# A streaming-encoder block: the memory's projections moved to the front, and one seven-product form for the whole first feed-forward

## The chip, the cores and the metric

The kernel runs on one core of one Trainium2 chip. The metric is the device time of one execution in microseconds (us). The kernel before takes 2411.06 us, the median of three runs (2410.53 to 2412.25). Of one execution there is also a trace from the hardware profiler, in which the core's engines are named PE (matrix products; its weight loads are PEld), DVE (the vector engine), ACT (the scalar engine), POOL and SP. SP issues most of the transfers from memory, POOL a few.

## The reference

One layer is computed, in float32, on 256 tokens of 2048 features (`x`), with 256 memory tokens (`mem`):

```
x += 1/2 * SwiGLU(norm(x))                                  # first feed-forward, 2048 -> 2 x 5632 -> 2048
proj = norm(x) @ w_in                                       # mixer: two recurrences and their gates
x += (sigmoid(gate_A)*y_A + sigmoid(gate_B)*y_B) @ w_out
h, m = norm(x), norm(mem)                                   # cross attention, 4 heads of 512
q = h @ wq ;  k, v = split(m @ wkv)
x += concat_heads(softmax(q k^T / sqrt(512)) v) @ wo
x += 1/2 * SwiGLU(norm(x))                                  # second feed-forward
out = norm(x)

SwiGLU(h): gate, up = split(h @ w_up);  (silu(gate) * up) @ w_down
```

The keys and values depend on `mem` and `wkv` alone, so their place in the program is free up to the attention.

## The kernel before

**Split products.** Each float32 operand is split into a high part, which PE multiplies at its fast rate, and a low part, the remainder. A product of two tiles is three matmuls (high by high, high by low, low by high). For each weight tile (128 x 2048, a *piece*, 1 MB) ACT copies out the high part (L154, `h`) and DVE subtracts it from the raw tile (L155, `l`). The results of matmuls, each 512 columns wide in the feed-forwards, gather in eight banks (`acc`).

**The feed-forward.** The hidden width of 5632 is cut into 11 groups of 512. A group's up-projection has eight pieces, p0 to p7, each of 256 input features by 1024 columns (gate and up). A piece covers a two by two block of tiles for each of the operands, and there are several forms for it:

- *plain* and *mixed*: eight products, 24 matmuls; DVE makes one low part of 2048 columns.
- *fast*: seven products, 21 matmuls, on sums and differences of the blocks (a scheme like Strassen's). The weights' differences are made first (L327 to L331 and L341, `td`); then the raw part of 1536 columns and two halves of the differences (1024 columns each) are split into high and low (L154, L155, `l` and `tl`).
- *fast early*: the same with the differences partly in the raw tile's place.
- *fast added*: as fast, but the low part of 1536 columns is made by ACT (the negated high part, L336) and an adding DMA of POOL, so that DVE makes only the differences and their low parts.
- *ready*: the differences were made earlier, kept in DRAM and come back by a DMA in place of a quarter of the raw piece. They are made by `make_ahead` beside other stages: a load by POOL into `prep`, four subtractions (L218), a store by POOL.

A group's down-projection has four pieces of 24 matmuls, each for a block of 512 output columns; some are *added* (DVE makes no low part for them). Groups 1 and 2 are accompanied by two down pieces each, later groups by four. At a group's end DVE and ACT add up the banks (L700 to L712), scale and multiply gate and up (L646), PE turns the result (eight transposes, L653), and ACT and DVE split it (L657, L658, `hidop`). A finished pair of output tiles is added to `x` on DVE (L728).

The table `FIRST` gives the forms and the order of the pieces of the first feed-forward: group 0 is plain, groups 1 and 2 are half mixed, group 3 has two mixed (their low part by an adding DMA), groups 4 to 10 are fast with four added. In the second, all pieces are fast but two of group 0, and `sums_ready` names 56 that are ready.

**The order.** One list, `plan`, holds every weight piece in the order in which PE uses it: first feed-forward, mixer (`in`, `v`, `gate`, `ab`, `out`), `q` (16 column pieces), `k` (16), `mv` (the values, 16 row pieces of 24 matmuls), `o` (16), second feed-forward. `weights` prepares up to two pieces ahead of their use, and `head`, `rest` and `beside` issue other work at given indices of the list: at the opening the operands of `x` are prepared with the first pieces. A column piece (`product`, L360 and L363) has 16 matmuls of 512 and 16 of 256 columns, and its result is summed by ACT (`lo`, L397) and DVE (L399). A row piece is `rows_product` (L385 to L388). Each engine executes its own instructions in the program's order, and waits in that order. The attention's scores and softmax run as generators that are pumped, a step at a time, beside the value pieces.

## Time and profile before

| | us |
|---|---|
| median of three runs | 2411.06 (2410.53 to 2412.25) |
| the profiled execution, its span | 2408.3 |
| PE busy | 2398.9 (100%) |
| DVE busy | 2049.8 (85%) |
| ACT busy | 1467.9 (61%) |
| POOL busy | 100.4 (4%) |

The span reaches from the first to the last instruction of the profiled execution; the median lies 2.76 us above it. A row of a group of instructions reads: line, engine, operation, result <- operands, shape, xcount | busy time in all, mean duration in ns | idle time before them and what ended it. A row of a timeline starts with the start and the duration in us. Durations of neighbouring instructions on PE and DVE overlap, so the distance between two starts is what an instruction occupies of its engine. Line numbers are those of the kernel whose profile is shown; after the change a line has another number (L154 and L155 become L147 and L148, L397 and L399 L407 and L409, L613 and L615 L603 and L605, L327 to L331 and L341 L334 to L338 and L348).

### The profile page before, as it was taken

Reading aid. Unit: us, or ns where it says so; the run is one execution under the profiler, and the core shown is the slowest. Engines: PE = TensorE matmul, PEld = TensorE weight load, DVE = VectorE, ACT = ScalarE, POOL = GpSimd, SP = SyncE. Lnnn points to the kernel's source line nnn. Section 1 sums busy time; section 2 is a strip of 40 time slices with the busy share of each in tenths; the row PEclk is TensorE's granted clock in tenths of the full one; section 3 lists DMA queues with packets and bytes.
Section 4 is the critical chain, followed back from the end, with each engine's and each line's share of the span. In section 5 each row is a group of like instructions: output and inputs, shape, how many; then the busy total and the mean of one; then the engine's idle time right before and its main releaser. Section 6 shows DMA issues by size and latency. Waiting matters only on the chain.

```text
span 2408.3 us, 30805 instructions
## 1 busy us (share of the span) xinstructions
PE 2398.9 (100%) x12098; PEld 2002.8 (83%) x12098; DVE 2049.8 (85%) x2291; ACT 1467.9 (61%) x1502; POOL 100.4 (4%) x162
## 2 busy tenths in 40 slices
PE   9999999999999999999999999999999999999998
PEld 8888888888888888888888888888888888888887
DVE  7999999999866878689777777677799999999995
ACT  8567777777654454476434555545676666666664
POOL 0000000000000000000000000000000000000000
PEclk9999999999999999999999999999999999999999
DMA  8578999999858776878999889876688877787873
GB/s 318 194 234 254 277 276 278 277 272 273 270 215 317 276 283 247 299 286 313 350 339 343 334 334 335 322 282 221 212 319 318 295 279 284 268 292 271 293 281 143
DMA packets 101666, 678.57 MB, mean 282 GB/s; under 512 B 11280, under 2 KB 11792, under 8 KB 29072
## 3 DMA queue, kind: packets, MB, share of 16 engines
q1 hardware_dynamic: 78624, 517.99, 57.7%
q0 software_dynamic: 22752, 158.35, 22.0%
q8 instruction: 95, 1.56, 0.3%
q14 instruction: 51, 0.42, 0.1%
q10 hardware_dynamic: 144, 0.26, 0.0%
HBM read 615.73 MB, written 60.82 MB: 281 GB/s over the span
## 4 chain that ended last, share of the span: by engine, by line
PE 98%; DVE 1%; DMA 0%; ACT 0%; issue 0%; ACTq 0%
PE acc L613 36%; PE acc L615 18%; PE acc L360 11%; PE acc L385 8%; PE acc L386 8%; PE acc L388 8%; PE acc L363 6%; PE acc L653 1%; PE acc L528 1%; DVE tl L155 0%; DVE l L155 0%; PE acc L989 0%; DMA raw<-wd 0%; PE acc L1288 0%; PE acc L1242 0%; PE acc L1104 0%
## 5 line engine op out<-in xcount | busy, mean ns | idle before, releaser
L154 ACT ACTIVATE h<-raw 128x2048 fp32r<-128x2048 f32 (+3 forms) x572 | 862.8, 1533 | 616.1 <-PE acc L386 217.7
L155 DVE TENSOR_TENSOR l<-raw,h 128x2048 fp32r<-128x2048 f32 (+2 forms) x405 | 832.7, 2058 | 226.0 <-ACT h L154 224.4
L613 PE MATMUL acc<-h,xh 128*128 128x512 f32 x1220 | 474.7, 391 | 0.1
L613 PE MATMUL acc<-h,xl 128*128 128x512 f32 x1220 | 472.7, 390 | 0.0
L613 PE MATMUL acc<-h,hidop 128*128 128x512 f32 x1408 | 352.6, 391 | 0.3 <-ACT h L154 0.3
L385 PE MATMUL acc<-h,ops 128*128 128x512 f32 x832 | 326.5, 392 | 0.0
L386 PE MATMUL acc<-h,ops 128*128 128x512 f32 x832 | 324.2, 390 | 0.0
L613 PEld LDWEIGHTS acc<-h,hidop 128*128 128x128 f32 x1408 | 262.5, 188 | 54.5 <-ACT h L154 1.0
L360 PE MATMUL acc<-ops,h 128*128 128x512 f32 x1152 | 277.6, 392 | 0.0
L613 PEld LDWEIGHTS acc<-h,xh 128*128 128x128 f32 x1220 | 229.0, 188 | 52.8 <-ACT h L154 4.7
L613 PEld LDWEIGHTS acc<-h,xl 128*128 128x128 f32 x1220 | 229.1, 188 | 46.5
L360 PEld LDWEIGHTS acc<-ops,h 128*128 128x128 f32 x1152 | 211.4, 188 | 41.4
L155 DVE TENSOR_TENSOR tl<-raw,h 128x1024 fp32r<-128x1024 f32 x167 | 197.4, 1217 | 12.1 <-ACT h L154 11.6
L154 ACT ACTIVATE h<-td 128x1024 fp32r<-128x1024 f32 x145 | 151.8, 1055 | 88.9 <-DVE td L327 35.3
L388 PE MATMUL acc<-l,ops 128*128 128x512 f32 x832 | 206.0, 389 | 0.0
L615 PE MATMUL acc<-l,hidop 128*128 128x512 f32 x704 | 190.6, 389 | 0.0
L385 PEld LDWEIGHTS acc<-h,ops 128*128 128x128 f32 x832 | 156.2, 188 | 32.3
L388 PEld LDWEIGHTS acc<-l,ops 128*128 128x128 f32 x832 | 156.1, 188 | 32.4
L155 DVE TENSOR_TENSOR tl<-td,h 128x1024 fp32r<-128x1024 f32 x145 | 175.9, 1218 | 8.3 <-ACT h L154 7.4
L386 PEld LDWEIGHTS acc<-h,ops 128*128 128x128 f32 x832 | 156.3, 188 | 31.4
L615 PE MATMUL acc<-tl,xh 128*128 128x512 f32 x624 | 177.4, 391 | 0.0
L615 PE MATMUL acc<-l,xh 128*128 128x512 f32 x600 | 165.1, 390 | 0.0
(264 smaller groups left out, 2487.7 us busy)
## 6 DMA issues: line engine op xcount, KB each, us to landing
raw<-wu SPq DMA_DIRECT2D x116, 1024.0 KB, 6.4
raw<-wd SPq DMA_DIRECT2D x88, 1024.0 KB, 6.8
prep<-wu POOLq DMA_DIRECT2D x56, 1024.0 KB, 6.8
t<-prep POOLq DMA_DIRECT2D x56, 1024.0 KB, 5.7
raw<-t SPq DMA_DIRECT2D x56, 1024.0 KB, 6.9
raw<-wu SPq DMA_DIRECT2D x56, 768.0 KB, 4.8
raw<-win SPq DMA_DIRECT2D x40, 1024.0 KB, 5.0
raw<-wg SPq DMA_DIRECT2D x32, 1024.0 KB, 5.5
```

The source lines that it names most:

```text
L154: done["high"] = act.activation(h, raw, ACT.Copy).ins
L155: done["low"] = dve.tensor_tensor(out=l, in0=raw, in1=h.bitcast(F32), op=ALU.subtract).ins
L360: pe.matmul(acc, h[:, k * P:(k + 1) * P], xs[k], start=k == 0, stop=False)
L363: done["product"] = pe.matmul(acc[:, :T], l[:, k * P:(k + 1) * P], xs[k][:, :T], start=False, stop=k == KT - 1).ins
L385: pe.matmul(accs[t], x[:, t * P:][:, :P], h[j], start=first and j == 0, stop=False)
L386: pe.matmul(accs[t], x[:, T + t * P:][:, :P], h[j], start=False, stop=False)
L388: done["product"] = pe.matmul(accs[t], x[:, t * P:][:, :P], l[j], start=False, stop=last and j == 3).ins
L528: pe.transpose(acc[:, z * T + t * P:][:, :P], tile[:, t * 512 + (2 * y + z) * P:][:, :P], ident)
L613: pe.matmul(acc, a, b, start=start, stop=False)
L615: pe.matmul(acc, ah, bl, start=False, stop=stop)
L653: pe.transpose(acc[:, z * T + t * P:][:, :P], hid[t][:, (2 * y + z) * P:][:, :P], ident)
```

## The change

The value and key products of the memory stand at the head of the plan. The memory's operands are prepared at the opening, in place of those of `x`; `x` is loaded and its pairs and sums are prepared behind the first value pieces. The keys, the values and the memory's scale are written to DRAM by POOL, and read back for each head in the attention. All 11 groups of the first feed-forward have the same order of fast and added pieces; in groups 1, 2 and 4 to 9 one fast piece is ready, its differences made beside the value and key products. The first two pieces are fast early. In the second feed-forward 50 pieces in place of 56 are ready. The attention of a head is pumped beside the query products and the output products, whose order (`OUT_ORDER`) lets the first two output blocks start before the last head is done. The pools of the first feed-forward change from three to four wide tiles.

```diff
-FIRST = [
-    "p0 p1 p2 p3 p4 p5 p6 p7",
-    "m0 f1 m2 f3 f5 m4 f7 m6",
-    "m0 f1 m2 f3 f5 m4 f7 m6",
-    "f1 f3 M0 f4 f2 M6 f5 f7",
-    "f1 a3 f0 a4 f2 a5 a6 f7",
...
-KINDS = {"p": "plain", "m": "mixed", "M": "mixed", "f": "fast", "a": "fast"}
+PIECES = "f1 a3 f0 a4 f2 a5 a6 f7"
+FIRST = [PIECES.replace("f2", "r2") if g in (1, 2, 4, 5, 6, 7, 8, 9) else PIECES for g in range(NG)]
...
 def sums_ready(name, e):
-    made = {0:(),1:(6,),2:(5,7),3:(5,7)}.get(e[1], (0, 5, 7) if e[1] % 2 else (0, 3, 5, 7))
+    if name == "ffn1":
+        return e[0] == "fast" and f"r{e[2]}" in FIRST[e[1]]
+    made = {0: (), 1: (5, 7), 2: (3, 5, 7), 3: (3, 5, 7)}.get(e[1], (0, 3, 5, 7))
     return name == "ffn2" and e[0] == "fast" and e[2] not in made
...
+    for g in range(4):
+        plan_rows("mv", wvm, g)
+    plan_columns("k", wk, range(KT))
+    first_ffn = len(plan)
     plan_ffn("ffn1", wu1, wd1)
...
     plan_columns("q", wq, range(KT))
-    plan_columns("k", wk, range(KT))
-    for name, w in (("mv", wvm), ("o", wo)):
-        for g in range(4):
-            plan_rows(name, w, g)
+    for g, kq in OUT_ORDER:
+        plan.append((("o", g, kq), wo[g, kq], "plain"))
...
+        if i < first_ffn:
+            if made_first:
+                turn[0] = i + 3 if len(made_first) > 1 else first_middle + 2
+                steps = make_ahead(*made_first.pop(0))
+                next(steps)
+                under_way.append((i + 2, steps))
...
+    rest[8] = load_vectors
+    for q in range(4):
+        rest[9 + 5 * q] = lambda q=q: load_x(q)
+        rest[11 + 5 * q] = lambda q=q: pairs_x(q)
+        rest[12 + 5 * q] = lambda q=q: (sums_x(0), load_residual(q))
+        rest[13 + 5 * q] = lambda: sums_x(1)
...
+    def keep_values():
+        if not root_of:
+            nc.gpsimd.dma_start(kept_r, sqm.rstd())
+            root_of["mem"] = sqm.rstd_tokens()
+        g, accs = values.pop(0)
+        for t in range(2):
+            f, s = slot(name="vf")[:, :512], slot(F32R, "vs")
+            act.activation(f, accs[t], ACT.Copy, scale=root_of["mem"][:, t:t + 1])
+            split(s[:, :512], s[:, 512:], f)
+            nc.gpsimd.dma_start(kept_v[2 * g + t], s)
+
+    with scope(mem=6, tmp=6, tmp2=1, norms=1, prep=1):
+        for g in range(4):
+            values.append((g, [bank(), bank()]))
+            for kq in range(4):
+                rows_product(values[-1][1], ms.tiles, weights("mv", g, kq), 4 * kq, kq == 0, kq == 3, g == kq == 0)
+            if g:
+                keep_values()
+        ks = Operands()
+        for m in range(KT):
+            ks.add(summed(product(ms.tiles, weights("k", m))[0]))
+            if not m:
+                keep_values()
+            if m % 2:
+                nc.gpsimd.dma_start(kept_k[m // 2], ks.cur)
+
     with scope(**FFN1_POOLS):
         ffn("ffn1", pairs1, sq1, to_mix)
```

The first place where the order moves is DVE's queue at the start of the first feed-forward. Before, the kernel opens with it: `raw` is a piece of weights, `xf` and `xg` are `x`, and each piece gives only its low part (L155).

```order
L300 TENSOR_SCALAR h_179<-raw_168 128x512
L753 SCALAR_TENSOR_TENSOR xl_175<-xf_172,xh_174 128x256
L302 TENSOR_TENSOR l_180<-raw_168,h_179 128x512
L155 TENSOR_TENSOR l_180<-raw_168,h_179 128x512
L753 SCALAR_TENSOR_TENSOR xl_175<-xf_172,xh_174 128x256
L155 TENSOR_TENSOR l_180<-raw_168,h_179 128x512 x2
L155 TENSOR_TENSOR xl_201<-xg_171,xh_200 128x512
L155 TENSOR_TENSOR l_206<-raw_204,h_205 128x512 x4
```

After the change it follows the last key column. `raw_1774` and `raw_1844` are the first two pieces, `acc_1790` is the bank of the last key column, and L409 and L433 make its sum and its low part.

```order
L336 TENSOR_TENSOR raw_1774<-raw_1774,td_1776 128x512
L148 TENSOR_TENSOR tl_1785<-td_1776,h_1784 128x1024
L348 TENSOR_TENSOR raw_1774<-raw_1774 128x512
L409 TENSOR_TENSOR sum_1825<-acc_1790,lo_1823 128x256
L336 TENSOR_TENSOR raw_1844<-raw_1844,td_1846 128x512
L148 TENSOR_TENSOR l_1850<-raw_1844,h_1849 128x1536
L148 TENSOR_TENSOR tl_1785<-raw_1774,h_1784 128x1024
L433 TENSOR_TENSOR ops_1771<-sum_1825,ops_1771 128x256
L348 TENSOR_TENSOR raw_1844<-raw_1844 128x512
L148 TENSOR_TENSOR tl_1855<-td_1846,h_1854 128x1024
L334 TENSOR_TENSOR td_1890<-raw_1888 128x1024
L148 TENSOR_TENSOR tl_1855<-raw_1844,h_1854 128x1024
```

The key column's sum stands in the queue ahead of the second low half of the first piece and of nearly all of the second piece's work.

The second place is DVE's queue where group 0 ends and group 1 begins. Before, group 0 is plain: its end (L646) stands among the last of `x`'s sums (L583, `xs`), and the next pieces are a fast and a mixed one (`raw_599`, `raw_670`).

```order
L327 TENSOR_TENSOR td_601<-raw_599 128x1024
L583 TENSOR_TENSOR xs_615<-xg_433 128x128
L329 TENSOR_TENSOR td_601<-raw_599,td_601 128x512
L583 TENSOR_TENSOR xs_615<-xg_433 128x128
L646 SCALAR_TENSOR_TENSOR ev_589<-acc_219,rtok_591,ev_589 128x512
L646 SCALAR_TENSOR_TENSOR ev_589<-acc_220,rtok_591,ev_589 128x512
L331 TENSOR_TENSOR td_601<-raw_599,td_601 128x512
L155 TENSOR_TENSOR tl_610<-td_601,h_609 128x1024
```

After the change, group 0 is fast and ends with the sums of its seven banks (L690 to L701):

```order
L338 TENSOR_TENSOR td_2112<-raw1_2110,td_2112 128x512
L690 TENSOR_TENSOR ev_2150<-acc_1865,ev_2150 128x512
L334 TENSOR_TENSOR td_2170<-raw_2168 128x1024
L148 TENSOR_TENSOR tl_2121<-td_2112,h_2120 128x1024
L512 RECIPROCAL rtok_2152<-stdt_2151 128x2
L691 TENSOR_TENSOR ev_2150<-acc_1864,ev_2150 128x512
L698 TENSOR_TENSOR ev_2150<-acc_1861,ev_2150 128x512
L698 TENSOR_TENSOR ev_2150<-acc_1863,ev_2150 128x512
L701 TENSOR_TENSOR ev_2150<-acc_1866,ev_2150 128x512
L698 TENSOR_TENSOR ev_2150<-acc_1862,ev_2150 128x512
L701 TENSOR_TENSOR ev_2150<-acc_1863,ev_2150 128x512
L636 SCALAR_TENSOR_TENSOR ev_2150<-ev_2150,rtok_2152 128x512 x2
```

Between the end of one piece's low parts and the next piece's differences there now stand seven additions that group 0 did not have before.

More of the change, by code (lines that the diff above doesn't have):

```diff
@@ L386, in rows_product @@
             pe.matmul(accs[t], x[:, T + t * P:][:, :P], h[j], start=False, stop=False)
-        for x, t, j in terms:
+            if by_tile and j < 3 and t:
+                for y in range(2):
+                    pe.matmul(accs[y], x[:, y * P:][:, :P], l[j], start=False, stop=False)
+        for x, t, j in terms[6:] if by_tile else terms:
             done["product"] = pe.matmul(accs[t], x[:, t * P:][:, :P], l[j], start=False, stop=last and j == 3).ins
@@ L470, in rstd_tokens @@
             return r
[L473 removed]
+    FFN1_POOLS = dict(wide=4, hd=1, raw1=1)
     FFN2_POOLS = dict(wide=2, raw2=2, hid=1, hd=1)
@@ L597, in block_kernel, with three @@
     held = []
-    def three(products, last=0, hold=False, early=0):
+    def three(products, last=0, hold=False):
         high = [(acc, ah, bh, start) for acc, (ah, al), (bh, bl), start, _ in products]
         low = [(acc, al, bh, False) for acc, (ah, al), (bh, bl), _, _ in products]
-        if early:
-            for i in range(0, len(high), 2):
-                for acc, a, b, start in high[i:i + 2] + low[i:i + 2]:
-                    pe.matmul(acc, a, b, start=start, stop=False)
-                if i < early:
-                    for acc, (ah, _), (_, bl), _, _ in products[i:i + 2]:
-                        pe.matmul(acc, ah, bl, start=False, stop=False)
-            high, low, products = [], [], products[early:]
         for acc, a, b, start in [m for pair in zip(high, low) for m in pair]:
@@ L785, in head_residual @@
-    def head_residual(i):
-        for c in (2 * i, 2 * i + 1):
-            for t in range(2):
-                sp.dma_start(xt[c][:, t * 512:(t + 1) * 512], xin[t * P:(t + 1) * P, c * 512:(c + 1) * 512])
-            sq1.add(c, by_vector=c == 3)
-        if i:
-            sp.dma_start(vt[:, small_n:NVEC], vec[:, small_n:])
-    head += [lambda p=p: head_x(p) for p in range(8)]
-    def early_sums():
-        scaled(xq[0][1], opening[0][:, 16:], gain1, 0)
-        for which in ((1, "sums"), (0, "less")):
-            sums1[0]((which,))
@@ L1297, in to_ffn @@
         out = []
-        sums2.append(operand_pairs(turned(xt[c]), gain2, c, slot(name="xg"), out, every=True))
+        sums2.append(operand_pairs(turned(xt[c]), gain2, c, slot(name="xg"), out, differences=True))
         pairs2.extend(out)
@@ L1308, in to_ffn_half @@
             out3.append([])
-        sums = operand_pairs(turned(xt[3], [y]), gain2, 3, *out3, every=True)
+        sums = operand_pairs(turned(xt[3], [y]), gain2, 3, *out3, differences=True)
         pairs2.append(out3[1][-1])
```

329 lines of the change are left out of this document (156 added, 173 removed), and 6 rows, old and new, of the table FIRST.

## The prediction

> **What bounds the kernel now.** I read the page's totals and slices first, then the waits of TensorE (PE), then the stretches of the first feed-forward, then single instructions.
>
> ```profile
> span 2408.3 us, 30805 instructions
> PE 2398.9 (100%) x12098; PEld 2002.8 (83%) x12098; DVE 2049.8 (85%) x2291; ACT 1467.9 (61%) x1502; POOL 100.4 (4%) x162
> PE   9999999999999999999999999999999999999998
> DVE  7999999999866878689777777677799999999995
> PEclk9999999999999999999999999999999999999999
> PE warm L143 <- DVE ones L140: 1.1, 1, 1.1
> PE acc L607 <- DVE h L300: 0.3, 1, 0.3
> PE acc L613 <- ACT h L154: 0.3, 1, 0.3
> ```
>
> PE is busy in every slice at full clock, and its three waits sum to 1.7 us. So time falls only by the matmuls that go away. The DVE row is nearly as full in both feed-forwards, and that is the second bound. The median of the runs, 2411.06, lies 2.76 above the profiled span, 2408.3; I sum against the span and add 2.76 at the end. Here are stretches of the first feed-forward (columns: length, PE, weight loads, DVE, ACT, POOL, clock, DMA share, GB/s), then two of the second:
>
> ```profile
> 60.00:107.00 47.00, 47.00 (x207) 38.46 (x207) 46.90 (x54) 25.82 (x22) 0.00 (x0) 1.00 0.54 202
> 107.00:166.00 59.00, 59.00 (x269) 48.57 (x268) 58.19 (x62) 36.59 (x32) 1.01 (x1) 1.00 0.61 203
> 226.00:287.00 61.00, 61.00 (x273) 49.84 (x272) 59.94 (x63) 46.02 (x39) 4.36 (x5) 1.00 0.90 275
> 287.00:348.00 61.00, 61.00 (x272) 49.96 (x271) 59.72 (x62) 44.14 (x37) 4.36 (x5) 1.00 0.92 276
> 1760.00:1820.00 60.00, 60.00 (x270) 49.59 (x270) 56.83 (x57) 40.68 (x38) 0.00 (x0) 1.00 0.83 308
> 1820.00:1880.00 60.00, 59.95 (x272) 49.30 (x271) 58.38 (x55) 41.59 (x39) 0.00 (x0) 1.00 0.81 303
> ```
>
> From 60 to 166 us (groups 1 and 2, four eight-product pieces and four seven-product pieces each) DVE is busy 105.1 of 106 us, and PE waits for nothing. Seven products there would give DVE more work and PE less time to hide it.
>
> **Prices.** A 512-column matmul costs PE its spacing, not its duration; from the chain of waits:
>
> ```profile
> 10.77 3.63 PE acc L613 x16
> 14.40 1.81 PE acc L615 x8
> ...
> 211.28 1.03 PE L653 MATMUL acc<-vt,ev 128*128 128x128 f32 x8
> 212.07 2.07 PE L613 MATMUL acc<-h,hidop 128*128 128x512 f32 x8
> ```
>
> 3.63/16 = 0.227 us; a piece of 24 is 5.45, one of 21 is 4.77. The 8 transposes of a group take 212.07 − 211.28 = 0.79. For DVE the starts of back-to-back instructions:
>
> ```profile
> 232.64 1.22 DVE L327 TENSOR_TENSOR td<-raw 128x1024 f32<-128x1024 f32 x1
> 233.77 1.75 DVE L155 TENSOR_TENSOR l<-raw,h 128x1536 fp32r<-128x1536 f32 x1
> 235.44 1.22 DVE L155 TENSOR_TENSOR tl<-td,h 128x1024 fp32r<-128x1024 f32 x1
> 236.58 0.69 DVE L329 TENSOR_TENSOR td<-raw,td 128x512 f32<-128x512 f32 x1
> 237.18 1.22 DVE L155 TENSOR_TENSOR tl<-td,h 128x1024 fp32r<-128x1024 f32 x1
> ...
> 254.54 2.28 DVE L155 TENSOR_TENSOR l<-raw,h 128x2048 fp32r<-128x2048 f32 x1
> 256.74 1.22 DVE L155 TENSOR_TENSOR tl<-td,h 128x1024 fp32r<-128x1024 f32 x1
> ```
>
> Start to start: 1.14 (1024 wide), 1.67 (1536), 0.60 (512), 2.20 (2048). A piece then costs DVE:
> - plain or mixed: one low part, 2.21
> - fast: differences 1.14 + 0.60 + 0.60, low parts 1.67 + 2 × 1.14, together 6.29
> - fast added (1536 low part left to POOL's DMA): 4.62
> - ready (differences loaded): 1.67 + 2.28 = 3.95
>
> A group's end adds seven sums (0.60) and two scaled products (0.66), 5.52, and two low parts of the turned hidden operand, 1.20: 6.72. Two finished output columns add four residual additions, 2.40. (Means of the groups below, less the 0.08 by which each start precedes the end before it.)
>
> ```profile
> L709 DVE TENSOR_TENSOR ev<-acc,ev 128x512 f32<-128x512 f32 x30 | 19.6, 680 | 0.0
> L646 DVE SCALAR_TENSOR_TENSOR hid<-hd,rtok,hid 128x512 f32<-128x512 f32 x22 | 15.4, 741 | 0.0
> L658 DVE TENSOR_TENSOR hidop<-acc,hidop 128x512 fp32r<-128x512 f32 x44 | 28.5, 682 | 1.2 <-ACT hidop L657 0.9
> L728 DVE SCALAR_TENSOR_TENSOR x<-acc,x 128x512 f32<-128x512 f32 x96 | 63.8, 682 | 23.0 <-PE acc L615 22.9
> ```
>
> Check on a steady group of before: 43.64 (four fast, four added) + 6.63 (three of four down pieces, one being added) + 6.72 + 2.40 = 59.39; the trace has 59.94 and 59.72.
>
> A page speaks against these prices: the Trainium skill, "VectorE: DVE Perf Modes", section "The DRAIN you can't avoid", says that the next instruction starts only when the pipe is empty, so the full durations (2.28 for 2.20, 1.22 for 1.14) would count. For some 213 instructions at about 0.08 that would be an estimated 17 us more stall. The spacing in these rows disagrees, and the row decides.
>
> **What the change removes.** Group 0 loses a product in 8 pieces, groups 1 and 2 in 4 each, group 3 in 2: 18 pieces × 3 = 54 matmuls × 0.227 = **−12.3 us** on PE, the binding engine. The memory's value and key products are moved, 32 pieces with the same matmuls: 0.
>
> **What it adds on DVE.** In the new order DVE's queue holds the sum of the last key column ahead of most of the second feed-forward piece's work. DVE goes in order, so however idle it was under the keys, it can begin the rest only when PE has finished that column, after ACT's copy (0.38) and DVE's sum (0.33):
>
> ```profile
> L397 ACT ACTIVATE lo<-acc 128x256 f32<-128x256 f32 x96 | 35.9, 377 | 6.8 <-PE acc L1243 6.1
> L399 DVE TENSOR_TENSOR sum<-acc,lo 128x256 f32<-128x256 f32 x72 | 29.6, 416 | 0.0
> ```
>
> From there to the last low part of group 3, DVE has: rest of the first two pieces 0.60 + 1.67 + 1.14 + 0.33 + 0.60 + 2.28 = 6.62, rest of group 0 (three fast, three added) 32.73, its end 6.72, group 1 (three fast, four added, one ready) 41.30, two down pieces with a group's end and residuals 13.54, group 2 41.30 + 13.54, group 3 (none ready) 43.64 and one down piece's low part 2.21: 201.6 us. PE needs in the same stretch three groups of 168 matmuls, 166 of group 3 up to that low part, and four down pieces of 24: 766, 173.9 us; three times 8 transposes, 2.4; and 16 matmuls of the next down piece, which its queue has ahead of that point, 3.6: 179.9 us. PE therefore waits 0.7 + 201.6 − 179.9 = **+22.4 us**, spread over groups 0 to 3 in steps below 2.7. I round to 22. In before, the plain group 0 (8 × 2.21 + 6.72 = 24.4 of DVE for 192 × 0.227 = 43.6 of PE) let DVE run ahead; that cover is gone.
>
> How this could be smaller: DVE's lead at a steady group's start was
>
> ```profile
> 211.71 2.36 DVE L155 TENSOR_TENSOR tl<-td,h 128x1024 fp32r<-128x1024 f32 x2 [0.85 <-ACT h L154]
> ...
> 221.46 0.84 PE L615 MATMUL acc<-tl,xh 128*128 128x512 f32 x3
> ...
> 258.19 0.63 PE L615 MATMUL acc<-tl,xh 128*128 128x512 f32 x2
> ```
>
> The first half, about 212.93, is used at 221.46: 8.5 us. At the group's end the low part that starts at 256.74 (above) ends at 257.96 and is used at 258.19: 0.2 us. So a lead is eaten within a group, and 8.5 us is the most that I can grant the new start.
>
> **From group 4 on** six of seven groups replace a fast piece by a ready one: DVE −2.34 each, and no matmul fewer; DVE is below PE there already, so 0. Their DMA grows by 0.75 MB:
>
> ```profile
> raw<-wu SPq DMA_DIRECT2D x116, 1024.0 KB, 6.4
> raw<-t SPq DMA_DIRECT2D x56, 1024.0 KB, 6.9
> raw<-wu SPq DMA_DIRECT2D x56, 768.0 KB, 4.8
> ```
>
> 1024 + 768 KB for 1024. That comes on 275 GB/s × 61 us = 16.8 MB: share 0.92 becomes about 0.96. I take 0; below a gain is excluded because PE doesn't wait, above it is 0.75 MB / 275 GB/s = 2.7 us per group where DMA ends last.
>
> **Second feed-forward.** Six fewer ready pieces, DVE +2.34 each, in different groups. The stretches above leave 3.2 and 1.6 us per 60: 0, with +3 as the upper bound (two groups, 0.75 each beyond the cover, and as much again).
>
> **Opening.** The first product stood at 4.69, and SP issues a transfer each 0.45 us:
>
> ```profile
> 1.18 0.42 SPq L298 DMA_DIRECT2D raw<-wu  x1
> 1.65 0.42 SPq L307 DMA_DIRECT2D xf<-xT  x1
> ...
> 4.69 1.05 PE L607 MATMUL acc<-h,xh 128*128 128x512 f32 x2 [0.28 <-DVE h L300]
> ```
>
> The second piece's first quarter is now SP's ninth transfer and not the seventh: up to 0.9 later. I take +0.5, from −0.5 to +2 (x no longer needs to be prepared there). **Attention** is issued beside the query and output products, a piece of 5.45 us between steps, as it was beside the value products, where PE never waited: 0, with +5.45 as the bound (one step left uncovered). Writing and reloading keys and values, 51 more POOL issues, waits behind nothing that PE needs soon: 0.
>
> **Sum:** 2408.3 − 12.3 + 22 + 0.5 = 2418.5, and with 2.76 the median is **2421 us**.
>
> **Rivals.**
> 1. *DVE is not the bound; the saving is kept.* PE waits for nothing in 60–166 with DVE at 99%, which shows that a full DVE alone doesn't stop PE. Then 2411.06 − 12.3 = 2399 (with the opening 2399.3). Against: 22 us of shortage needs a lead that large, and the largest seen is 8.5. Chance 0.06.
> 2. *The first pieces come in with the full lead.* DVE has 5.45 us per piece under values and keys for some 3 us of work, and the first two pieces are loaded early. If the sum cost it nothing, the stall is 22 − 8.5 = 13.5: 2411.06 − 12.3 + 13.5 + 0.5 = 2413 (within). Against: the order of its queue. Chance 0.10.
> 3. *DMA ends last in the groups with ready pieces.* At a share of 0.96, if three of them lose 2.7 us: 2421 + 8 = 2429. Before reached 0.92 with no wait. Chance 0.08.
> 4. *The stalls slow PE's clock.* Before never idles, so its full PEclk row can't tell. If two pieces of 21 matmuls ran at half speed, 2 × 4.77: 2421 + 9.5 = 2430.5. The stalls are below 2.7 us each, so I don't expect it. The Trainium skill, "TensorE: Matmul & The Clock Gate", section "HAM oscillation — how this bites in real kernels", tells of such slowing when waits cross an activity window, given as about 3.4 us; no run shown so far can show it. Chance 0.04.
>
> The forecast has the rest, 0.72. About 0.2%, 4.8 us, is what a measurement of this kernel can tell from no change. Faster: rival 1, 0.06. Within: rival 2, 0.10. Slower: 0.84. The range runs from rival 2's price to just above rival 4's, 2413 to 2431; it leaves out rival 1 and the edges of the rest.
>
> **What would show it.** PE's matmuls 54 fewer. Keys and values take 16 × 5.45 = 87 and, with 16 narrow matmuls beside 16 wide ones, 16 × (3.63 + 16 × 1.43/12) = 89 us:
>
> ```profile
> 700.74 1.43 PE acc L363 x12
> ```
>
> So group 0 starts near 182; from there to about 400 PE should wait some 22 us in all for DVE's low parts, with DVE above 98% busy, and no waits in groups 4 to 10, in attention or in the second feed-forward. If PE waits less than 7 us there, the ledger is wrong and the change is faster (12.3 − 0.5 − 7 = 4.8); if it waits for DMA or after 400 us, a rival is right.

## The result and the profile after

The changed kernel takes **2520.33 us** (median of four runs, 2518.23 to 2524.96), the kernel before 2410.97: a ratio of 1.0456, 95% interval 1.0443 to 1.0469. It is slower by 109 us. The forecast was 2421, with 2413 to 2431 as its range: the sign was right, the size too small by a factor of eleven (109 us for 10).

The changed kernel's page, its totals and rows by slice:

```profile
span 2520.2 us, 30931 instructions
PE 2423.2 (96%) x12044; PEld 2004.1 (80%) x12044; DVE 2100.6 (83%) x2359; ACT 1505.3 (60%) x1549; POOL 131.7 (5%) x213
PE   9977888999999999999999999999999999999998
DVE  6568788989999986777878877787799999999995
PEclk9988899999999999999999999999999999999999
```

54 matmuls are gone (12098 to 12044), and yet PE is busy 24 us longer; its row has holes in the first eighth, where the clock row falls to 8, and DVE is less full there than it was. What PE waited for, over the whole span, the longest (us in total, times, longest):

```profile
PE acc L605 <- DMA l<-wu: 24.3, 6, 5.8
PE acc L603 <- ACT h L147: 15.2, 23, 1.6
PE acc L367 <- ACT h L147: 10.0, 1, 10.0
PE acc L603 <- DVE td L334: 9.0, 1, 9.0
PE acc L370 <- DVE l L148: 8.4, 3, 5.2
PE acc L605 <- DVE l L148: 7.0, 7, 1.4
PE acc L392 <- ACT h L147: 4.4, 1, 4.4
```

Before, all waits came to 1.7 us. L392 is a value product and L367 and L370 are key products, so the loss begins ahead of the feed-forward. Stage by stage, from the first and last matmul of each in the two timelines (the 176.1 us of values and keys, worked out in the prediction's last part as 87 + 89, are taken from before's middle):

| stage | before | after | difference |
|---|---|---|---|
| value and key products | 176.1 | 4.7 to 213.1: 208.4 | +32.3 |
| first feed-forward | 687.0 | 749.3 | +62.3 |
| mixer and attention, without the above | 859.8 | 867.5 | +7.7 |
| second feed-forward | 672.5 | 682.2 | +9.7 |

The sum is 112.0, the spans differ by 111.9. The stretches in which most of it lies (length, PE, weight loads, DVE, ACT, POOL, clock, DMA share, GB/s):

```profile
0.00:90.00 90.00, 84.11 (x361) 69.52 (x362) 60.41 (x86) 62.90 (x104) 4.65 (x12) 0.96 0.89 326
90.00:213.00 123.00, 104.56 (x555) 90.15 (x555) 78.55 (x108) 52.46 (x72) 12.25 (x23) 0.93 0.80 295
213.00:290.00 77.00, 57.71 (x217) 42.46 (x215) 63.62 (x73) 44.35 (x43) 4.56 (x6) 0.87 0.70 213
290.00:410.00 120.00, 101.10 (x419) 79.76 (x420) 104.39 (x110) 76.10 (x67) 6.94 (x8) 0.94 0.76 234
```

The prediction's ledger assumed that DVE works without a pause from the last key column to group 3. From 213 to 410 us it is idle for 13.4 and 15.6 us. Two places show what holds it. The first is DVE's timeline at the end of the keys, and PE's behind it:

```profile
207.26 1.76 DVE L148 TENSOR_TENSOR l<-raw,h 128x1536 fp32r<-128x1536 f32 x1 [0.95 <-ACT h L147]
218.12 1.42 DVE L213 TENSOR_TENSOR prep<-prep 128x512 f32<-128x512 f32 x2 [7.85 <-DMA prep<-wu]
219.46 0.42 DVE L409 TENSOR_TENSOR sum<-acc,lo 128x256 f32<-128x256 f32 x1
221.32 2.35 DVE L334 TENSOR_TENSOR td<-raw 128x1024 f32<-128x1024 f32 x2
...
214.28 0.39 PE L603 MATMUL acc<-h,xl 128*128 128x512 f32 x1
223.68 0.79 PE L603 MATMUL acc<-h,xh 128*128 128x512 f32 x1 [9.01 <-DVE td L334]
```

The last preparation's subtraction stands in DVE's queue ahead of the last key column's sum and of the first feed-forward's differences, and its load has not landed: DVE stands for 7.85 us, PE for 9.01. The second place is in group 2; PE, then POOL, then DVE:

```profile
364.22 0.39 PE L603 MATMUL acc<-h,xl 128*128 128x512 f32 x1
370.38 1.65 PE L605 MATMUL acc<-l,xh 128*128 128x512 f32 x3 [5.78 <-DMA l<-wu]
371.83 1.05 PE L605 MATMUL acc<-tl,xh 128*128 128x512 f32 x2
...
366.03 0.87 POOL L344 DMA_DIRECT2D l<-wu  x1 [5.80 <-ACT l L343]
...
374.53 2.36 DVE L148 TENSOR_TENSOR tl<-td,h 128x1024 fp32r<-128x1024 f32 x2 [6.53 <-ACT h L147]
```

An added piece's low part is issued at 366.03, after PE already needed it (364.6), and PE waits until it lands. DVE has run dry meanwhile, 6.53 us up to 374.53. The three matmuls after the wait take 1.45 us to the next start, where 0.68 is usual. The granted clock of these 2 us (the column before the last two) is 0.50:

```profile
370.40:372.40 2.00, 2.00 (x5) 1.61 (x6) 0.00 (x0) 0.34 (x1) 0.00 (x0) 0.50 1.05 279
```

### The profile page after: what moved, and what is told of

It reads as the page before. It is cut to its first block, busy times and chain, and to the rows that moved or that the text cites. A ratio compares the mean times of both kernels' runs of the same rounds, so it can differ in the third digit from the quotient of the medians.

```text
span 2520.2 us, 30931 instructions
## 1 busy us (share of the span) xinstructions
PE 2423.2 (96%) x12044; PEld 2004.1 (80%) x12044; DVE 2100.6 (83%) x2359; ACT 1505.3 (60%) x1549; POOL 131.7 (5%) x213
## 4 chain that ended last, share of the span: by engine, by line
PE 64%; DVE 8%; DMA 6%; issue 4%; ACT 3%; POOL 0%; ACTq 0%; DVEq 0%; POOLq 0%; SPq 0%
PE acc L603 22%; PE acc L605 11%; PE acc L367 8%; PE acc L398 6%; PE acc L392 6%; PE acc L393 6%; PE acc L370 4%; DMA raw<-wu 3%; DVE l L148 3%; DVE tl L148 2%; ACT h L147 2%; DMA l<-wu 1%; DMA td<-t 1%; PE acc L539 1%; PE acc L643 0%
## 5 line engine op out<-in xcount | busy, mean ns | idle before, releaser
L147 ACT ACTIVATE h<-raw 128x2048 fp32r<-128x2048 f32 (+3 forms) x558 | 835.3, 1522 | 616.8 <-PE acc L393 160.4
L148 DVE TENSOR_TENSOR l<-raw,h 128x2048 fp32r<-128x2048 f32 (+2 forms) x392 | 801.0, 2046 | 206.6 <-ACT h L147 205.8
L603 PE MATMUL acc<-h,xh 128*128 128x512 f32 x1230 | 486.1, 397 | 25.8 <-ACT h L147 15.2
L392 PE MATMUL acc<-h,ops 128*128 128x512 f32 x704 | 276.3, 392 | 0.0
L393 PE MATMUL acc<-h,ops 128*128 128x512 f32 x704 | 274.2, 389 | 0.0
L148 DVE TENSOR_TENSOR tl<-td,h 128x1024 fp32r<-128x1024 f32 x182 | 220.6, 1218 | 52.2 <-ACT h L147 51.7
L147 ACT ACTIVATE h<-td 128x1024 fp32r<-128x1024 f32 x182 | 190.0, 1054 | 112.5 <-PE acc L603 37.0
L367 PE MATMUL acc<-ops,h 128*128 128x512 f32 x896 | 219.1, 395 | 0.0
L213 DVE TENSOR_TENSOR prep<-prep 128x512 f32<-128x512 f32 x232 | 158.4, 687 | 48.6 <-DMA prep<-wu 45.1
L367 PEld LDWEIGHTS acc<-ops,h 128*128 128x128 f32 x896 | 165.6, 190 | 33.3
L605 PE MATMUL acc<-l,xh 128*128 128x512 f32 x534 | 158.8, 402 | 31.3 <-DMA l<-wu 24.3
L398 PE MATMUL acc<-l,ops 128*128 128x512 f32 x704 | 174.1, 389 | 0.8 <-DVE l L148 0.8
L605 PEld LDWEIGHTS acc<-tl,xh 128*128 128x128 f32 x696 | 131.0, 190 | 32.3 <-DVE tl L148 5.6
```

Of the source, the lines that this page charges most:

```text
L147: done["high"] = act.activation(h, raw, ACT.Copy).ins
L148: done["low"] = dve.tensor_tensor(out=l, in0=raw, in1=h.bitcast(F32), op=ALU.subtract).ins
L213: dve.tensor_tensor(out=b[o], in0=b[x], in1=b[y], op=ALU.subtract)
L367: pe.matmul(acc, h[:, k * P:(k + 1) * P], xs[k], start=k == 0, stop=False)
L392: pe.matmul(accs[t], x[:, t * P:][:, :P], h[j], start=first and j == 0, stop=False)
L393: pe.matmul(accs[t], x[:, T + t * P:][:, :P], h[j], start=False, stop=False)
```

## The experiments

Each time is one run beside a run of before (2409 to 2412 us), since the differences in question are from 5 to 90 us. "Keys end" is the start of the first feed-forward's first product, due at 181; "five groups" is the time from there to the transposes that end group 4's stretch, whose matmuls alone take 256 us in the change (267.9 in before, less the 12.3 saved), 261 in e4 and 272 in e7 and e9; "middle" is the mixer and the attention.

| kernel | us | keys end | five groups | rest of first feed-forward's groups | middle | second feed-forward |
|---|---|---|---|---|---|---|
| before | 2411 | – | 267.9 | 367.4 | 859.8 | 672.5 |
| the change | 2520.3 | 213.1 | 322.5 | 375.1 | 867.5 | 682.2 |
| e1 no ready piece | 2473.5 | 183.0 | 310.1 | 368.4 | 867.5 | 682.9 |
| e2 no subtraction | 2508.7 | 210.5 | 308.8 | 374.9 | 867.8 | 685.1 |
| e3 no adding | 2515.9 | 209.5 | 318.5 | 375.0 | 867.1 | 684.1 |
| e4 group 0 plain | 2498.5 | 212.1 | 298.6 | 375.1 | 865.6 | 685.5 |
| e7 groups 0 to 2 plain | 2437.1 | 182.5 | 272.2 | 367.3 | 867.7 | 685.6 |
| e9 as e7, 56 ready | 2428.9 | 185.9 | 278.8 | 367.2 | 859.7 | 675.4 |
| e11 e1, no adding | 2471.0 | 183.8 | 309.6 | 367.5 | 865.9 | 682.0 |

### The value and key products

e1 takes the ready pieces of the first feed-forward away, and with them the eight preparations:

```diff
-FIRST = [PIECES.replace("f2", "r2") if g in (1, 2, 4, 5, 6, 7, 8, 9) else PIECES for g in range(NG)]
+FIRST = [PIECES for g in range(NG)]
...
-    turn = [8]
+    turn = [first_middle + 2]
```

> The change, but no piece of the first feed-forward is ready: f2 stands in all groups, so the eight loads, subtractions and stores beside the value and key products go away. The preparation blames the value and key stage's loss (the first feed-forward's first product stands at 213 us, where 181 was due) on these eight pieces: the stage ends near 183, the steady groups 4 to 9 lose their 7.7 us over before, and groups 1 and 2 get 2.3 us of DVE work each: 2520 - 30 - 8 + 5 = about 2487. If the stage's loss is the move itself (operands of the memory and of x in one stretch, keys and values written), it stays: about 2515.

Measured 2473.51: 47 us less, where 33 were expected. The keys end at 183.0 (due 181), the groups from 5 on are back at 368.4 (before 367.4), and the wait at the first differences is gone. So the ready pieces cost 30 us beside the keys, some 12 at the start of group 0 and 6.7 in the steady groups, all of which the prediction had at nothing. The move itself costs about 2 us.

Where the 30 us lie shows in the change's trace. Up to 213 us PE waits four times: 4.44 us at 11.0, 2.78 at 129.4, 5.16 at 163.0 and 9.97 at 188.9; e1 has no wait above 0.3 us there. At the first, POOL has issued the first preparation's load at 1.28 us, beside the opening's transfers: SP's 256 KB loads of weights take 8.5 us to land in the first 12 us (median; 5.4 in e1). All eleven runs with a load by POOL at 1.28 us have such a wait, of 1.8 to 4.6 us; e1, e5, e7 and e11, without it, have none above 0.8. The other three have one shape, here the longest, on DVE, ACT and PE:

```profile
182.71 0.69 DVE L213 TENSOR_TENSOR prep<-prep 128x512 f32<-128x512 f32 x1 [11.10 <-DMA prep<-wu]
183.32 0.42 DVE L409 TENSOR_TENSOR sum<-acc,lo 128x256 f32<-128x256 f32 x1
...
183.77 0.42 ACT L432 ACTIVATE ops<-sum 128x256 fp32r<-128x256 f32 x1 [14.21 <-DVE sum L409]
186.99 1.90 ACT L147 ACTIVATE h<-raw 128x2048 fp32r<-128x2048 f32 x1
...
188.94 3.35 PE L367 MATMUL acc<-ms,h 128*128 128x512 f32 x7 [9.97 <-ACT h L147]
```

A preparation's first subtraction (L213) stands in DVE's queue until its load has landed, 11.10 us here and 7.24 and 7.34 before the two others. Behind it stands a key column's sum (L409), ACT waits for that sum with its low part (L432), and behind this stands the high part (L147) that PE needs.

e2 leaves the four subtractions out beside the keys, so the data of eight ready pieces are not the differences.

```diff
-            for o, x, y in ((1, 0, 1), (0, 0, 2), (2, 2, 1), (3, 3, 2)):
+            for o, x, y in () if not subtract else ((1, 0, 1), (0, 0, 2), (2, 2, 1), (3, 3, 2)):
...
-                steps = make_ahead(*made_first.pop(0))
+                steps = make_ahead(*made_first.pop(0), subtract=False)
```

> The change, but beside the value and key products the eight pieces are only loaded and stored again, without the four subtractions (so the eight ready pieces get wrong differences). The transfers stay as they are. If DVE's queue is held up by waiting for the loads, the stage ends near 185 and the time is about 2492. If the transfers themselves take the memory's bandwidth from the weights, the stage still ends near 213 and the time stays within 5 us of 2520.

Measured 2508.65, and the keys still end at 210.5, where 185 was expected if DVE's waiting held them up. But this is no proof that the transfers do. DVE's waits for a load are gone, and others stand in their place: PE waits 6.02 us at 110.1 and 6.64 at 141.6. POOL now waits for each load before it stores, with the stores of the values behind that in its queue, and ACT stands 11.4 us until one of them has landed. SP's queue has a load of the first feed-forward ahead of three key pieces, and stands 17.3 us until a preparation's store has landed. So the two causes stay unseparated here. What e2 does show is the start of group 0: without subtractions the group takes 61.6 us instead of 73.6. e10 gives the stage a fourth raw buffer:

```diff
-    with scope(mem=6, tmp=6, tmp2=1, norms=1, prep=1):
+    with scope(mem=4, tmp=6, tmp2=1, norms=1, prep=1, raw1=1):
```

> The change, with one raw buffer more beside the value and key products (four in place of three; two of the memory's operand tiles move to the general slots). If the stage waits for weights because a transfer can only be issued when DVE frees a buffer, and then takes 7 us to land, a fourth buffer hides more of it: the stage ends near 200 instead of 213, 2507. If the 16 engines are at their limit (308 GB/s over the stage), it stays within 5 us of 2520.

Measured 2520.93: the keys end at 209.4, 4 us earlier, and the five groups take 7 us more. No gain. e14 and e15 issue 8 and 16 loads of 1 MB whose data nobody uses, in e1:

```diff
+            for _ in range(2):      # e14: 1
+                t = scoped["prep"].tile([P, 2048], F32, name="prep", tag="prep")
+                nc.gpsimd.dma_start(t, wu1[i % 8, 2])
```

> As e1 (no ready piece in the first feed-forward; 2473.5, the stage ends at 183.0), with eight loads of 1 MB by POOL beside the value and key products whose data nobody uses: no subtraction, no store. If the amount moved counts, 8 MB cost what four preparations did, 9 us: the stage ends near 192. If it is the stores, or the round trip of load and store, it ends near 183.

> As e14 with sixteen such loads, 16 MB, as much as the eight preparations of the change move. If the amount moved counts, the stage ends near 213; if the stores do, near 183 to 190.

Measured 2477.89 with the keys' end at 187.6, and 2502.71 with 214.4. Sixteen loads without a store end the stage where eight loads and eight stores do. The stretches of e1, then of e14, then two of e15:

```profile
0.00:40.00 40.00, 38.31 (x165) 31.21 (x166) 32.24 (x54) 31.19 (x55) 0.20 (x4) 1.00 0.90 322
40.00:183.00 143.00, 143.00 (x754) 123.47 (x753) 94.77 (x119) 89.30 (x124) 8.73 (x16) 1.00 0.78 276
```

```profile
0.00:40.00 40.00, 36.37 (x144) 28.38 (x145) 24.59 (x44) 25.58 (x49) 3.02 (x9) 0.96 0.98 382
40.00:187.00 147.00, 147.00 (x768) 126.63 (x768) 102.02 (x129) 93.84 (x130) 10.14 (x19) 1.00 0.85 310
```

```profile
40.00:100.00 60.00, 60.00 (x268) 49.72 (x268) 38.01 (x40) 38.96 (x58) 5.34 (x10) 1.00 1.00 380
100.00:120.00 20.00, 12.46 (x56) 10.14 (x55) 9.06 (x10) 7.87 (x7) 2.14 (x4) 0.83 0.79 264
```

In e14 all of the 4.6 us are lost in the first 40 us; then PE waits for nothing over 147 us, at a mean share of 0.85 and 310 GB/s, more than the change has from 90 to 213 us (0.80, 295). In e15 PE even works 60 us without a wait at a share of 1.00, and loses most of its time where the share is lower. These are its waits from 90 us on, and SP's:

```profile
PE acc L366 <- ACT h L147: 18.3, 2, 10.8
ACT vs L147 <- DMA v<-vs: 10.9, 1, 10.9
SPq L323 <- DMA v<-vs: 21.7, 1, 21.7
```

POOL has one buffer for its loads, so each waits for the one before, and the stores of the values stand behind them. ACT stands 10.9 us until such a store has landed; SP stands 21.7 us at a load of the first feed-forward, with three key pieces behind it. From 145 us on PE doesn't wait any more. So e15 comes to the change's end by another way, and the two runs don't show that the amount moved counts. What is shown: the preparations cost 30 us (e1), eight loads without subtraction and store 4.6 (e14), and in the change 22.4 us of PE's waits stand behind a preparation's load. How much of it the transfers' own slowness makes (a preparation's load takes 8.1 us to land in this stage, 6.8 over the span) stays open.

e6 has four ready pieces, in groups 0 to 3, prepared late in the stage:

```diff
-FIRST = [PIECES.replace("f2", "r2") if g in (1, 2, 4, 5, 6, 7, 8, 9) else PIECES for g in range(NG)]
+FIRST = [PIECES.replace("f2", "r2") if g < 4 else PIECES for g in range(NG)]
...
-    turn = [8]
+    turn = [20]
```

> As the change, but only groups 0 to 3 have a ready piece (f2), four in all, prepared late beside the key products. By the ledger each takes 2.34 us from DVE where it is short: 2473.5 (e1) - 9.4 = 2464. If 8 MB of transfers beside the keys still hold up the weights as 16 MB did (30 us), the stage ends near 198 instead of 183, and the time is about 2480.

Measured 2488.97: the keys end at 191.6, and the wait for `td` at group 0's start is back, 10.2 us. Neither number of the expectation fits, the second comes nearer: putting the ready pieces where DVE is short does not pay for their preparation.

### Groups 0 to 3: DVE's work or the adding DMA

e3 makes the added pieces of groups 0 to 3 fast, so DVE does their low part:

```diff
+FIRST = [f.replace("a", "f") if g < 4 else f for g, f in enumerate(FIRST)]
```

> The change, with all added pieces of groups 0 to 3 made fast: DVE makes their 1536 columns of low part, and there is no adding DMA. By DVE's ledger each costs 1.67 more in a stretch where DVE is short: 16 x 1.67 = 27 us more, 2547. If instead the landing of the adding DMA, which has no lead to hide it, ends last (PE waits 21 us for it in groups 0 to 3), these waits go and the time falls: 2520 - 21 + 5 = about 2504.

Measured 2515.86, between the two and nearer to neither: PE's wait for `l<-wu` falls from 24.3 to 5.8 us, and others take its place (its feed-forward products wait 27.4 us for ACT's high parts, 15.2 in the change). Giving DVE 27 us more work costs nothing, since it removes as much waiting for DMA. e11 does the same without the ready pieces, so that DVE's own work is all that is left:

> As e1 (no ready piece in the first feed-forward), with the added pieces of groups 0 to 3 made fast, so that neither the transfers beside the keys nor the adding DMA can stop PE there. What is left is DVE's own work: by the ledger a stall of 22 + 4.7 (two ready pieces less) + 26.7 (16 pieces of 1.67) = 53 us over groups 0 to 3, and since it comes in short waits, no slow clock. The first products of group 0 to the end of group 4 then take 256 + 53 = 309 us, the whole as e1, 2474. If DVE's prices are too high or DVE isn't the bound there, it falls below 2455.

Measured 2470.96, and the five groups take 309.6 us where 309 was expected. Its stretches, and below them one place of 4 us and its waits from 184 to 495 us:

```profile
184.00:300.00 116.00, 100.07 (x398) 72.42 (x397) 115.33 (x120) 66.19 (x62) 0.53 (x1) 0.99 0.46 168
300.00:430.00 130.00, 113.04 (x465) 83.45 (x466) 129.97 (x132) 75.68 (x66) 0.89 (x1) 1.00 0.53 180
```

```profile
243.00:247.00 4.00, 3.97 (x11) 3.11 (x12) 4.00 (x6) 2.41 (x2) 0.00 (x0) 0.59 0.07 14
PE acc L603 <- ACT h L147: 17.1, 33, 1.7
PE acc L605 <- DVE l L148: 13.8, 20, 1.5
PE acc L605 <- DMA l<-wu: 1.8, 1, 1.8
```

DVE is busy 245.3 of 246 us, PE waits in many pieces of 1.8 us at most, and the clock stays at 0.99 to 1.00 but for the one place shown. Here the ledger holds to a microsecond: DVE is the bound of these groups, and its spacing prices are right. That also decides against the rule of the Trainium skill ("VectorE: DVE Perf Modes", section "The DRAIN you can't avoid") that the prediction weighed: with an estimated 17 us more it would have been 326.

e1 against e11 shows the other half. With the adding DMA DVE's ledger is 26.7 us shorter (283 us expected for the five groups), and they take 310.1: as long as without it. So the adding DMA takes back all that it saves DVE, by waits of 5 us and the slow clock after them.

e4 makes group 0 plain, e7 groups 0 to 2 without ready pieces:

```diff
+FIRST[0] = "p0 p1 p2 p3 p4 p5 p6 p7"                                             # e4
+FIRST = ["p0 p1 p2 p3 p4 p5 p6 p7"] * 3 + [PIECES] * (NG - 3)                    # e7
-    return [("fast", g, int(e[1])) for e in FIRST[g].split()]
+    return [("plain" if e[0] == "p" else "fast", g, int(e[1])) for e in FIRST[g].split()]
```

> The change, with group 0 in eight plain pieces as before (24 matmuls more, 5.4 us). By the ledger DVE loses some 22 us of work in group 0 and with it that group's stall (28.7 us against before in the trace) and part of group 1's: 2520 - 29 + 5 - 5 = about 2491. If group 0's stall comes from weights that land late behind the value and key stage, it stays by more than half: 2505 or more.

> As e1, with groups 0 to 2 in eight plain pieces: 72 matmuls more than e1 (16.3 us), 18 more than before. DVE then has 24.4 us of work per group for 44 of PE. If the stalls of groups 0 to 4 (54 us in e1) are DVE's shortage and what follows from it, they go: 2473.5 + 16.3 - 54 = about 2436, which leaves the mixer's and the second feed-forward's losses. If the stalls come with the moved stage itself, groups 0 to 2 still show waits of several us each, 2450 or more.

e4 measured 2498.47, between its two numbers: group 0 gains 17.8, group 1 6.0, groups 2 and 3 nothing, so the lead lasts for one group. e7 measured 2437.06, as expected, and its five groups take what their matmuls take:

```profile
182.00:232.00 50.00, 50.00 (x227) 41.51 (x226) 22.94 (x15) 21.51 (x16) 0.53 (x1) 1.00 0.59 207
232.00:290.00 58.00, 58.00 (x264) 48.18 (x263) 30.78 (x21) 22.49 (x16) 0.00 (x0) 1.00 0.53 187
290.00:345.00 55.00, 55.00 (x246) 45.55 (x245) 32.61 (x27) 24.44 (x19) 1.76 (x2) 1.00 0.58 187
```

No wait above 0.8 us is left, DVE is about half idle, and 18 matmuls more than before cost their 4 us. The keys' move takes nothing from the feed-forward: its stalls come with the seven products in groups 0 to 2, and what is left of them in the change comes with the ready pieces.

### The second feed-forward, the middle, and versions that follow

e5 sets before's 56 ready pieces of the second feed-forward into e1, with other turns beside the mixer and the attention:

```diff
-    made = {0: (), 1: (5, 7), 2: (3, 5, 7), 3: (3, 5, 7)}.get(e[1], (0, 3, 5, 7))
+    made = {0: (), 1: (6,), 2: (5, 7), 3: (5, 7)}.get(e[1], (0, 5, 7) if e[1] % 2 else (0, 3, 5, 7))
...
-            turn[0] = i + (3 if early or len(made_ahead) % 3 else 2)
+            turn[0] = i + (3 + len(made_ahead) % 2 if early else 2)
```

> As e1 (no ready piece in the first feed-forward, 2473.5), and in the second feed-forward the 56 ready pieces of before in place of 50; for that the preparation's turns beside the mixer and the attention lie at other indices. If the second feed-forward's loss (682.9 us against 672.5) comes from the six pieces, it goes: 2463, and with the 3.9 us wait at the mixer's first small products, behind a preparation's subtractions, 2459. By the ledger of the prediction (second feed-forward free) the six pieces cost nothing, and the time stays at 2473.

Measured 2505.45, far above all three numbers of the expectation. The second feed-forward falls from e1's 682.9 us to 675.4, so the six pieces cost 7.5 us there. But the preparations then crowd the middle, 906.9 instead of 867.5: PE waits 24.7 us for the residual (`L539 <- DVE x L1199`) behind them. e9 takes e7 and runs eight of the 56 preparations beside the plain groups, where DVE has time:

```diff
-    FFN1_POOLS = dict(wide=4, hd=1, raw1=1)
+    FFN1_POOLS = dict(wide=3, hd=1, raw1=1, prep=1)
...
+        elif made_ahead and i < first_middle:
+            turn[0] = i + 3 if i < first_ffn + 22 else first_middle + 2
+            steps = make_ahead(*made_ahead.pop(0))
+            next(steps)
+            under_way.append((i + 2, steps))
```

> As e7 (groups 0 to 2 plain, 2437), with 56 ready pieces in the second feed-forward; eight of the 56 preparations run beside groups 0 to 2 of the first feed-forward, where DVE has 20 us to spare per group, the other 48 beside the mixer and the attention (e7: 50). If the second feed-forward's loss is the six pieces and the mixer's and attention's loss is DVE's load of preparations, both shrink: 685.6 to about 675 and 867.7 to about 862: 2437 - 11 - 6 = 2420. If the middle's loss belongs to the attention's new place, it stays: 2426.

Measured 2428.89. The middle takes 859.7 us, before's time to 0.1, and the second feed-forward 675.4: both losses came with the preparations, the middle's with their crowding, not with the attention's new place. 9 us are missing against the forecast: the five groups grew by 6.6 with the preparations beside them, and the keys' end moved by 3.4, since the first preparation's load stands in the opening here too (PE waits 1.86 us at 8.5). 2.9 us in the second feed-forward stay unexplained. This is the fastest version with the keys in front, and it is 19 us slower than the run of before beside it (2410.02).

e8 has group 0 plain, two ready pieces in groups 1 and 2, and e5's 56 ready ones with its turns; e12 is e9 with seven products in group 2, two of its pieces ready, and 54 ready ones:

```diff
+FIRST = ["p0 p1 p2 p3 p4 p5 p6 p7"] + [PIECES.replace("f2", "r2").replace("f0", "r0")] * 2 + [PIECES] * (NG - 3)     # e8
+FIRST = ["p0 p1 p2 p3 p4 p5 p6 p7"] * 2 + [PIECES.replace("f2", "r2").replace("f0", "r0")] + [PIECES] * (NG - 3)     # e12
```

> A version that follows from the ledger: group 0 plain, two ready pieces in each of groups 1 and 2 (four in all, prepared late beside the keys), no other ready piece in the first feed-forward, 56 in the second. By the ledger no group is short of DVE: 2408.3 - 12.3 + 5.4 + 2 (keys) + 4 (mixer) + 3 = 2410, about 2412 with the median. If the adding DMA's landing still stops PE in groups 1 and 2, with its slow clock after it, about 15 us more, 2427.

> As e9, but group 2 has seven products in all pieces, two of them ready (prepared beside group 0), and 54 pieces are ready in the second feed-forward. 24 matmuls fewer than e9 (5.4 us). DVE has some 52.5 us of work in group 2 for 49.9 of PE, which the lead from the plain groups covers: 2420 - 5 = 2415. If the added pieces' DMA stops PE as soon as the lead is gone, two waits of 5 us and the slow clock after them: 2427.

Measured 2508.14 and 2482.16. e8 loses 50 us in the crowded middle like e5, and its groups 1 to 3 still take 59 to 61 us. In e12 group 2 alone takes 77.2 us; over the span PE waits 19.8 us for ACT's high parts of the feed-forwards' pieces, up to 8.3 at once. In group 2 ACT stands 8.85 and 6.75 us until the differences of the two ready pieces (`td<-t`) have landed, and PE waits 14.2 us behind it. Both missed their forecasts (2412 or 2427, 2415 or 2427) by far: work that is balanced in the ledger's sum was still late in place.

### The price of a long wait

e13 is the kernel before, with seven waits in the key products:

```diff
+        if m > 1 and m % 2 == 0:
+            idle = bank("idle")
+            pe.matmul(idle[:, :P], ones, ones, start=True, stop=True)
+            for _ in range(3 * m):
+                dve.memset(ones, 1.0)
+            idle = bank("idle")
+            pe.matmul(idle[:, :P], ones, ones, start=True, stop=True)
         acc = two_ahead(ms.tiles, "k", m, 0)
```

> The kernel before, with seven waits of PE put in front of every second key product: a chain of 6, 12, ... 42 small DVE instructions that PE must wait for, about 1.5 to 9 us. If a long wait slows PE's clock, the matmuls behind the longer ones (4.5 us and more in the change) run at 0.45 us in place of 0.23 for some 2 to 3 us of loss each, and behind those below 3 us there are none. If the slow matmuls in the change had another cause (transfers, or the form of the pieces), all of them run at 0.23 here, and only the waits themselves, some 35 us, add up.

Measured 2499.91; the waits came out longer than meant, 6.0 to 15.2 us, 72.3 in sum, since DVE had other work between the small instructions.

```profile
PE idle L1233 <- DVE ones L1231: 72.3, 7, 15.2
1475.33 0.77 PE L1233 MATMUL idle<-ones 128*128 128x128 f32 x2 [6.05 <-DVE ones L1231]
1475.74 5.48 PE L360 MATMUL acc<-ops,h 128*128 128x512 f32 x15
```

The key product of 15 matmuls behind the shortest wait takes 5.48 us; before, 16 take 3.92. Behind each of the seven waits 5 to 10 matmuls start 0.43 us apart instead of 0.23, all within 4.8 us, which costs some 1 to 2 us; the longest wait, 15.2 us, has the fewest behind it. In the change some 90 matmuls run so, which costs about 18 us (before and e11 have fewer than 20); behind each of its eight waits of 4.4 us and more there are 5 to 12. For shorter waits the length alone does not decide: one of 2.67 us in the change (561.8) has seven behind it, e1's of 1.79 and 1.81 us have none, and behind e11's of 1.68 us at 243.0, which several shorter ones precede, seven start 0.43 us apart. That is the place with the clock of 0.59.

## Why the prediction was wrong

**The bound and the direction: right.** PE gives back only the matmuls that go, and DVE is the bound of groups 0 to 3: e7 shows that the stall comes with the seven products there, e11 that the ledger's prices and its sum hold to 1 us where DVE alone decides. Rival 1 is out.

**"Moved, 32 pieces with the same matmuls: 0": wrong by 32 us.** I priced the move by PE and left out what is issued beside it: eight preparations, each a load, four subtractions and a store, in a stage that was to take 176 us. I read the DMA share for groups 4 to 9 only, and did not ask which queue stands still until a preparation's load has landed. In the trace DVE's queue does, for 7 to 11 us at a time, and three waits of PE follow (17.9 us); a fourth, 4.4 us, is in the opening. Without the preparations (e1) 2 of the 32 us are left. Which part of the 30 the amount moved has is not shown.

**"PE waits +22 us": 67 in the trace (322.5 − 256).** The ledger is a lower bound, not the stall. It adds up DVE's work and lets DVE wait for nothing after the last key column. It waits for a preparation's load at group 0's start (without the subtractions, e2, the group is 12 us shorter), and it runs dry behind the adding DMA in each of groups 0 to 3. I took "fast added" as 1.67 us of relief per piece. Its landing was hidden in before by the lead; I had the lead's end in the quoted rows (0.2 us) and did not ask what else the lead covered. What replaces the step: the stall of these groups is DVE's ledger plus every latency that stood under the lead.

**Steps "below 2.7 us", so no slow clock (rival 4, 0.04): wrong.** In groups 0 to 3 five waits of PE are of 4.5 to 9.0 us, and over the span some 90 matmuls run at about half speed, which costs 18 us. The mechanism was described, its condition misjudged, since it follows from the steps above. The Trainium skill, "TensorE: Matmul & The Clock Gate", section "HAM oscillation — how this bites in real kernels", agrees in kind: waits that cross its window cost a slow start. e13 gives the size here, 1 to 2 us for each; as a limit the page's 3.4 us does not hold here, since the waits of 2.67 and 1.68 us above had slow matmuls behind them too.

**Ready pieces in groups 4 to 9: 0, found 7.** 375.1 against 368.4 in e1. Rival 3, at 8 us, has about the size; of its mechanism one place is seen. Half of the loss, 3.3 us, lies in group 5, behind one wait of 2.67 us for an added piece's landing and its slow matmuls. The rest is 0.1 to 1.1 us in each of the other five groups, without a wait above 1.02 us.

**Second feed-forward: 0, at most 3, found 9.7.** Six fewer ready pieces are 14 us of DVE work in groups with 1.6 to 3.2 us to spare per 60; I counted two groups. e5 and e9, with all 56, are at 675.4 and return about 7 of it.

**Attention: 0, found 7.7 in the middle.** Not uncovered steps, but 50 preparations in a shorter middle (e9: 859.7 with 48 and other turns). **Opening: +0.5, at most +2.** In e1 opening and keys' stage together are about 2 us late, inside the bound. In the change the wait of 4.44 us at 11.0 us is outside it: the term counted the place of SP's transfers, and not POOL's 1 MB load beside them.

## What to carry to other kernels

A ledger of the second-busiest engine gives the least that a change can cost; to forecast the cost, list also every transfer and every in-order neighbour that the old slack covered, because all of them come out when the lead is gone. A stage is priced by all that is issued beside it: before calling a move free, ask of every added transfer which queues stand still until it lands, and what stands behind in them. Work made "ahead" in an idle stage must not stand at the head of an in-order queue while its load is still on the way. And a run that leaves a part out can bring new waits of its own: read where its time goes before taking its total as the answer.

## What the runs showed of the hardware

In e13 and in the change, a wait of PE of 4.4 us or more cost, beside itself, 5 to 12 matmuls at 0.43 us in place of 0.23, some 1 to 2.5 us, whatever its length up to 15.2 us; of waits between 1.6 and 1.8 us most cost nothing more, and one did (e11). In the opening, one load of 1 MB beside the first weights went with a wait of PE of 1.8 to 4.6 us (eleven runs). Behind the opening, transfers beside a stage of weights did not stop PE by their amount alone: it ran 60 us without a wait at a mean share of 1.00 of the 16 engines (e15) and 147 us at 0.85 (e14). What stopped it there was an engine's queue that stood 7 to 22 us until one transfer had landed. And two ways of giving DVE relief (an adding DMA, differences made ahead) had a net worth of about zero or less where no lead was left to hide their landing.
